# Add and tanh-GELU on one core: one ScalarE pass over z instead of an Abs, a GELU and a VectorE step, with larger rows for the transfers

## The chip, the cores and the metric

The kernel runs on one core of one Trainium2 chip. The metric is the time in microseconds (us) of one execution on the device. Engines are named as the profile names them: DVE is VectorE, ACT is ScalarE, POOL is GpSimd, SP is SyncE, which here only issues DMAs. PE, the matmul engine, has no work.

## The reference

```python
def setup_inputs():
    batch, dim = 1024, 4096
    return {"x": randn(batch, dim) as float32, "y": randn(batch, dim) as float32}

def reference(x, y):
    z = x + y
    return (0.5 * z * (1 + np.tanh(np.sqrt(2 / np.pi) * (z + 0.044715 * z ** 3)))).astype(np.float32)
```

Each input and the output are 16.8 MB, so 50.3 MB move in one execution.

## The kernel before

Each of the 128 partitions holds 8 consecutive rows of the matrices, 32768 fp32 elements or 128 KB. A single tile `z` of that size holds x, then z = x + y, then the result, all in place. y passes through a two-buffer pool of 8192 elements each.

The work is cut into 16 chunks of 2048 elements. For each chunk there are four steps. `add` (line 150) adds y into z, on DVE for the six chunks in `by_dve` and on POOL for the other ten. `mag` (line 155) writes |z| into PSUM on ACT. `gelu` (line 158) replaces it in PSUM by GELU(-|z|), also on ACT. `end` (line 167) adds max(z, 0) and that PSUM tile into z on DVE, by the identity GELU(z) = max(z, 0) + GELU(-|z|). Two PSUM tiles take turns, so `mag` of a chunk waits for `end` of the chunk two before.

All transfers are issued by SP in the order of the list `sp`, and its instructions wait in that order: y0, x0, y1, x1, y2, y3, then three stores. A transfer of y has 8192 elements of each partition (rows of 32 KB, 4 MB in all), one of x 16384 (64 KB, 8 MB); the stores have 16384, 10240 and 6144 (64, 40 and 24 KB). y2 and y3 reuse the two y buffers and wait for the four adds that read the buffer before. The first store waits, beside its own data, for the first half of `end` of chunk 8 (`FIRST`), by a dependency added by hand. The order on POOL, ACT and DVE is written out in the lists `pool`, `acts` and `dve`; each engine works through its list in order.

At the start a one-column activation makes the GELU table load early. `begin_early` moves the first two DMA issues (y0 and x0) ahead of the program's start barrier, and `wait_late` moves the wait for the last store behind the closing barrier; both are the same in the two kernels.

Of the kernel before, what the change touches and what calls it, by code (L numbers as in the profile page):

```python
# [8 lines left out]
def begin_early(nc, count):  # L9


    head, body = (b.instructions for b in nc.main_func.blocks[:2])
    SP = mybir.EngineType.SP
    moved = [i for i in body if i.engine == SP and isinstance(i, mybir.InstDMACopy)][:count]
    assert not any(i.sync_info and i.sync_info.on_wait for i in moved)
    assert all(i.regs_accessed() == ((), ()) for i in moved)
    at = next(k for k, i in enumerate(head) if i.engine == SP)
    for k, i in enumerate(moved):
        body.remove(i)
        head.insert(at + k, i)  # L20


def wait_late(nc):

    body, end = (b.instructions for b in nc.main_func.blocks[1:3])
    last = [i for i in body if isinstance(i, mybir.InstDMACopy)][-1]
    (sem,) = [u.id for u in last.sync_info.on_update]
    all_done = end[0]  # L30
    reset = next(i for i in end if isinstance(i, mybir.InstDrain) and i.is_reset_sema)
    at = end.index(reset)
    clear = end[at + 1]
    first, stop = reset.reset_range_start, reset.reset_range_stop
    assert all_done.engine == mybir.EngineType.SP and reset.engine == mybir.EngineType.Pool
    assert isinstance(clear, mybir.InstISA) and clear.engine == mybir.EngineType.Pool
    waits = all_done.sync_info.on_wait
    (its,) = [w for w in waits if w.id == sem]

    end[0] = mybir.InstDrain(  # L40
        name=all_done.name, engine=all_done.engine, debug=all_done.debug, is_reset_sema=False,
        sync_info=mybir.SyncInfo(on_wait=[w for w in waits if w.id != sem], on_update=[]),
    )
    parts = []
    for f, e in ((first, sem), (sem + 1, stop)):
        if f < e:
            nc.gpsimd.sem_clear(range(f, e))
            parts.append(nc.cur_bb.bb.instructions.pop())
    end[at + 1 : at + 2] = parts
    end.append(  # L50
        mybir.InstEventSemaphore(
            name=clear.name, engine=mybir.EngineType.Activation, debug=clear.debug,
            sync_info=mybir.SyncInfo(
                on_wait=[its],
                on_update=[
                    mybir.SyncUpdate(
                        sync_type="semaphore", id=sem, ant_name=its.ant_name,
                        update_mode="sem-sub-imm", update_value=its.wait_value,
                    )
                ],  # L60
            ),
        )
    )


@with_exitstack
def kernel(
    ctx: ExitStack,
    tc: tile.TileContext,
    x: bass.AP,  # L70
    y: bass.AP,
    out: bass.AP,
):

    nc = tc.nc
    P = nc.NUM_PARTITIONS
    fp32 = mybir.dt.float32
    act = mybir.ActivationFunctionType
    alu = mybir.AluOpType

    N, D = x.shape
    assert N % P == 0
    TOT = N // P * D  # L90
    xv, yv, ov = (a.rearrange("(p n) d -> p (n d)", p=P) for a in (x, y, out))

    YS = 8192
    CH = 2048
    PS = 2
    xloads = [16384, 16384]
    yloads = [8192, 8192, 8192, 8192]
    FIRST = 8
    stores = [16384, 10240, 6144]

    def ranges(sizes):
        ends = [sum(sizes[: i + 1]) for i in range(len(sizes))]
        assert ends[-1] == TOT
        return [(e - f, e) for e, f in zip(ends, sizes)]

    xr, yr, sr, cr = (ranges(r) for r in (xloads, yloads, stores, [CH] * (TOT // CH)))
    C = len(cr)

    by_dve = {0: 0, 2: 0, 4: 2, 6: 4, 8: 8, 12: 10}

    def over(rs, lo, hi):
        return [i for i, (a, b) in enumerate(rs) if a < hi and b > lo]

    pool_sb = ctx.enter_context(tc.tile_pool(name="xz", bufs=1))
    pool_y = ctx.enter_context(tc.tile_pool(name="y", bufs=2))
    pool_w = ctx.enter_context(
        tc.tile_pool(name="w", bufs=PS, space=bass.MemoryType.PSUM)
    )

    one = pool_sb.tile([P, 992], fp32, tag="one", name="one")  # L120
    zt = pool_sb.tile([P, TOT], fp32, tag="z", name="z")
    yt, wt, ends = {}, {}, {}

    def load_x(i):
        a, b = xr[i]
        nc.sync.dma_start(out=zt[:, a:b], in_=xv[:, a:b])

    def load_y(i):
        a, b = yr[i]
        s, o = divmod(a, YS)  # L130
        if o == 0:
            yt[s] = pool_y.tile([P, YS], fp32, tag="y", name=f"y{s}")
        nc.sync.dma_start(out=yt[s][:, o : o + b - a], in_=yv[:, a:b])  # L133

    def store(i):
        a, b = sr[i]
        ins = nc.sync.dma_start(out=ov[:, a:b], in_=zt[:, a:b])
        if i == 0:
            tc.add_manual_dep(
                ins.ins,  # L140
                ends[FIRST].name,
                mybir.DependencyInfo(mybir.DependencyClass.Sync, mybir.DependencyReason.DATA),
                reason="the stores join the queue when the last load is nearly done",
            )

    def add(c):
        a, b = cr[c]
        s, o = divmod(a, YS)
        eng = nc.vector if c in by_dve else nc.gpsimd
        eng.tensor_add(out=zt[:, a:b], in0=zt[:, a:b], in1=yt[s][:, o : o + b - a])  # L150

    def mag(c):
        a, b = cr[c]
        wt[c] = pool_w.tile([P, CH], fp32, tag="w", name=f"w{c}")
        nc.scalar.activation(out=wt[c], in_=zt[:, a:b], func=act.Abs)  # L155

    def gelu(c):
        nc.scalar.activation(  # L158
            out=wt[c], in_=wt[c], func=act.Gelu_apprx_tanh, scale=-1.0
        )  # L160

    def end(c):
        a, b = cr[c]
        parts = 2 if c == FIRST else 1
        n = (b - a) // parts
        for o in range(0, b - a, n):
            ins = nc.vector.scalar_tensor_tensor(  # L167
                out=zt[:, a + o : a + o + n], in0=zt[:, a + o : a + o + n], scalar=0.0,
                in1=wt[c][:, o : o + n], op0=alu.max, op1=alu.add,
            )  # L170
            ends.setdefault(c, ins.ins)


    sp = [(load_y, 0), (load_x, 0), (load_y, 1), (load_x, 1), (load_y, 2), (load_y, 3)]
    sp += [(store, i) for i in range(len(stores))]
    pool = [(add, c) for c in range(C) if c not in by_dve]
    dve, acts = [], []
    for c in range(C):
        dve += [(add, k) for k in sorted(by_dve) if by_dve[k] == c] + [(end, c)]
        acts += [(mag, c), (gelu, c)]  # L180

    needs = {
        load_x: lambda i: [],
        load_y: lambda i: [
            (add, c) for c in over(cr, yr[i][0] - 2 * YS, yr[i][1] - 2 * YS)
        ],
        add: lambda c: [(load_x, i) for i in over(xr, *cr[c])]
        + [(load_y, i) for i in over(yr, *cr[c])],
        mag: lambda c: [(add, c)] + ([(end, c - PS)] if c >= PS else []),
        gelu: lambda c: [(mag, c)],  # L190
        end: lambda c: [(gelu, c)],
        store: lambda i: [(end, c) for c in over(cr, *sr[i])] + [(end, FIRST)],
    }
    queues = [sp, pool, acts, dve]
    done = set()
    with tc.manual_schedule():
        nc.vector.memset(one[:, :1], 0.0)  # L197
        nc.scalar.activation(out=one[:, :1], in_=one[:, :1], func=act.Gelu_apprx_tanh)  # L198
        while any(queues):
            moved = False  # L200
            for q in queues:
                while q and all(n in done for n in needs[q[0][0]](q[0][1])):
                    fn, arg = q.pop(0)
                    fn(arg)
                    done.add((fn, arg))
                    moved = True
                    if q is not sp:
                        break
            assert moved, [q[:1] for q in queues]

    ctx.close()
    tc.close()
    tc.compile()  # L213
    begin_early(nc, 2)
    wait_late(nc)
# [30 lines left out]
```

## Time and profile before

| | before |
|---|---|
| time, median of 3 runs | 119.97 us |
| lowest and highest of the 3 | 119.97 and 120.43 us |
| span of the profiled execution, first to last instruction | 118.5 us |
| time of the profiled execution itself | not listed apart from the three runs; their median lies 1.45 us above its span |
| busy: DVE, ACT, POOL | 59.8, 60.8, 55.5 us |
| DMA queue: bytes, mean rate | 50.33 MB, 425 GB/s |

A line of a group has: the source line, the engine, the operation, what it writes and reads with the shapes, the number of instructions, then busy time and the mean of one in ns, then the idle time of that engine just ahead of these instructions and what ended it. A line of the order in time has: start, duration, engine, source line and operation, and in brackets the idle time before it. A line of waits has: who waited for whom, the sum in us, the number of times, the longest. The DMA line shows the span in 40 equal slices, each digit the busy share of the 16 DMA engines in tenths. A DMA of this kernel is cut into 128 packets, one for each partition's row, 8 for each of the 16 DMA engines; the trace also has each packet's start and duration. All transfers go through one queue.

### The profile page before, as it was taken

Reading aid. Unit: us, or ns where it says so; the run is one execution under the profiler, and the core shown is the slowest. Engines: PE = TensorE matmul, PEld = TensorE weight load, DVE = VectorE, ACT = ScalarE, POOL = GpSimd, SP = SyncE. Lnnn points to the kernel's source line nnn. Section 1 sums busy time; section 2 is a strip of 40 time slices with the busy share of each in tenths; the row PEclk is TensorE's granted clock in tenths of the full one; section 3 lists DMA queues with packets and bytes.
Section 4 is the critical chain, followed back from the end, with each engine's and each line's share of the span. In section 5 each row is a group of like instructions: output and inputs, shape, how many; then the busy total and the mean of one; then the engine's idle time right before and its main releaser. Section 6 shows DMA issues by size and latency. Waiting matters only on the chain.

```text
span 118.5 us, 160 instructions
## 1 busy us (share of the span) xinstructions
DVE 59.8 (50%) x24; ACT 60.8 (51%) x34; POOL 55.5 (47%) x14
## 2 busy tenths in 40 slices
DVE  0000000000399999699994594257999457742000
ACT  5000000000057989999369805797798999940000
POOL 0000000000399999998000029999999999100000
DMA  6989888998889988988899898998899889999996
GB/s 199 509 365 697 354 354 354 663 398 354 354 376 509 531 354 354 686 376 354 354 398 487 365 520 354 531 531 354 354 531 531 354 354 442 442 442 442 390 406 265
DMA packets 1296, 50.33 MB, mean 425 GB/s; under 512 B 144, under 2 KB 144, under 8 KB 144
## 3 DMA queue, kind: packets, MB, share of 16 engines
q1 hardware_dynamic: 1296, 50.33, 98.7%
HBM read 33.55 MB, written 16.78 MB: 425 GB/s over the span
## 4 chain that ended last, share of the span: by engine, by line
DMA 48%; POOL 34%; POOLq 4%; ACT 3%; DVE 2%; issue 0%; SPq 0%; DVEq 0%
POOL z L150 34%; DMA z<-in_x_dram 26%; DMA y<-in_y_dram 21%; POOLq L213 4%; DVE z L167 2%; ACT w L155 2%; ACT w L158 2%; SPq L133 0%; POOLq L150 0%; DVEq L167 0%
## 5 line engine op out<-in xcount | busy, mean ns | idle before, releaser
L150 POOL TENSOR_TENSOR z<-z,y 128x2048 f32<-128x2048 f32 x10 | 55.3, 5556 | 45.6 <-DMA z<-in_x_dram 31.1
L155 ACT ACTIVATE w<-z 128x2048 f32<-128x2048 f32 x16 | 30.1, 1880 | 42.5 <-DVE z L150 36.0
L167 DVE SCALAR_TENSOR_TENSOR z<-z,w 128x2048 f32<-128x2048 f32 (+1 forms) x17 | 36.3, 2155 | 16.0 <-ACT w L158 16.0
L150 DVE TENSOR_TENSOR z<-z,y 128x2048 f32<-128x2048 f32 x6 | 23.9, 4004 | 30.4 <-DMA z<-in_x_dram 30.1
L158 ACT ACTIVATE w<-w 128x2048 f32<-128x2048 f32 x16 | 29.8, 1862 | 0.5
L198 ACT ACT_TABLE_LOAD x1 | 1.3, 1283 | 1.3 <-PEq L230 1.3
L197 DVE MEMSET one<- 128x1 f32 x1 | 0.1, 59 | 1.3 <-PEq L230 1.3
L198 ACT ACTIVATE one<-one 128x1 f32<-128x1 f32 x1 | 0.2, 203 | 0.0
L230 POOL MEMSET const-float32-0.0<- 128x1 f32 x1 | 0.1, 100 | 0.2 <-issue 0.2
L230 POOL MEMSET const-uint8-127<- 128x1 uint8 x1 | 0.1, 103 | 0.0
L230 POOL MEMSET const-bfloat16-1.0<- 128x1 bf16 x1 | 0.1, 102 | 0.0
L230 POOL MEMSET const-float32-1.0<- 128x1 f32 x1 | 0.1, 100 | 0.0
## 6 DMA issues: line engine op xcount, KB each, us to landing
y<-in_y_dram SPq DMA_DIRECT2D x4, 4096.0 KB, 23.6
out_dram<-z SPq DMA_DIRECT2D x1, 5120.0 KB, 14.9
out_dram<-z SPq DMA_DIRECT2D x1, 3072.0 KB, 10.9
z<-in_x_dram SPq DMA_DIRECT2D x2, 44.9
out_dram<-z SPq DMA_DIRECT2D x1, 21.5
```

The source lines that it names most:

```text
L150: eng.tensor_add(out=zt[:, a:b], in0=zt[:, a:b], in1=yt[s][:, o : o + b - a])
L155: nc.scalar.activation(out=wt[c], in_=zt[:, a:b], func=act.Abs)
L158: nc.scalar.activation(out=wt[c], in_=wt[c], func=act.Gelu_apprx_tanh, scale=-1.0)
L167: ins = nc.vector.scalar_tensor_tensor(out=zt[:, a + o : a + o + n], in0=zt[:, a + o : a + o + n], scalar=0.0, in1=wt[c][:, o : o + n], op ...
L197: nc.vector.memset(one[:, :1], 0.0)
L198: nc.scalar.activation(out=one[:, :1], in_=one[:, :1], func=act.Gelu_apprx_tanh)
L213: tc.compile()
L230: nc = _bacc.Bacc("TRN2", target_bir_lowering=False, num_devices=1)
```

## The change

The steps `mag` and `end` are gone. `gelu` is one activation of ScalarE over z itself, from SBUF to SBUF, in place. All adds are on DVE but that of chunk 16, the last 2048 elements, which is on POOL. Of chunks 9 and 10, ACT copies x into PSUM (`to_psum`) when x1 has landed, and their adds on DVE take x from there. The last quarter's chunks are 2048, 2048, 1024, 1024 and 2048 elements, and ACT takes the chunks of the second half in the order 8, 9, 10, 11, 16, 12, 13, 14, 15.

y has one buffer of 16384 elements. y0 and y1 fill its two halves with rows of 32 KB; y2 has rows of 64 KB, fills all of it again, and so waits for adds 0 to 7. The order on SP is y0, y1, x0, x1, y2, store 0, store 1, each store with rows of 64 KB (8 MB). Store 0 waits for gelus 0 to 7 and nothing else (`GATE` is None); store 1 waits for all gelus of the second half. The two issues ahead of the start barrier are now y0 and y1.

```diff
-    YS = 8192
-    CH = 2048
-    PS = 2
-    xloads = [16384, 16384]
-    yloads = [8192, 8192, 8192, 8192]
-    FIRST = 8
-    stores = [16384, 10240, 6144]
+    HALF = TOT // 2
+    xloads = [HALF, HALF]
+    yloads = [8192, 8192, 16384]
+    stores = [16384, 16384]
+    chunks = [2048] * 14 + [1024, 1024, 2048]
+    by_pool = [16]
+    in_psum = [9, 10]
+    GATE = None
...
-    by_dve = {0: 0, 2: 0, 4: 2, 6: 4, 8: 8, 12: 10}
+    second = next(c for c in range(C) if cr[c][0] == HALF)
...
+    yt = pool_y.tile([P, HALF], fp32, tag="y", name="y")
+    xp, adds = {}, {}
...
     def load_y(i):
         a, b = yr[i]
-        s, o = divmod(a, YS)
-        if o == 0:
-            yt[s] = pool_y.tile([P, YS], fp32, tag="y", name=f"y{s}")
-        nc.sync.dma_start(out=yt[s][:, o : o + b - a], in_=yv[:, a:b])
+        o = a % HALF
+        nc.sync.dma_start(out=yt[:, o : o + b - a], in_=yv[:, a:b])
...
+    def to_psum(c):
+        a, b = cr[c]
+        xp[c] = pool_ps.tile([P, 2048], fp32, tag="xp", name=f"xp{c}")
+        nc.scalar.copy(out=xp[c][:, : b - a], in_=zt[:, a:b])
+
     def add(c):
         a, b = cr[c]
-        s, o = divmod(a, YS)
-        eng = nc.vector if c in by_dve else nc.gpsimd
-        eng.tensor_add(out=zt[:, a:b], in0=zt[:, a:b], in1=yt[s][:, o : o + b - a])
-
-    def mag(c):
+        o = a % HALF
+        eng = nc.gpsimd if c in by_pool else nc.vector
+        first = xp[c][:, : b - a] if c in in_psum else zt[:, a:b]
+        ins = eng.tensor_add(out=zt[:, a:b], in0=first, in1=yt[:, o : o + b - a])
+        adds[c] = ins.ins
+
+    def gelu(c):
         a, b = cr[c]
-        wt[c] = pool_w.tile([P, CH], fp32, tag="w", name=f"w{c}")
-        nc.scalar.activation(out=wt[c], in_=zt[:, a:b], func=act.Abs)
-
-    def gelu(c):
-        nc.scalar.activation(
-            out=wt[c], in_=wt[c], func=act.Gelu_apprx_tanh, scale=-1.0
-        )
-
-    def end(c):
...
+        nc.scalar.activation(out=zt[:, a:b], in_=zt[:, a:b], func=act.Gelu_apprx_tanh)
 
-    sp = [(load_y, 0), (load_x, 0), (load_y, 1), (load_x, 1), (load_y, 2), (load_y, 3)]
+    sp = [(load_y, i) for i in over(yr, 0, HALF)] + [(load_x, 0), (load_x, 1)]
+    sp += [(load_y, i) for i in over(yr, HALF, TOT)]
     sp += [(store, i) for i in range(len(stores))]
-    pool = [(add, c) for c in range(C) if c not in by_dve]
-    dve, acts = [], []
-    for c in range(C):
-        dve += [(add, k) for k in sorted(by_dve) if by_dve[k] == c] + [(end, c)]
-        acts += [(mag, c), (gelu, c)]
+    pool = [(add, c) for c in by_pool]
+    dve = [(add, c) for c in range(C) if c not in by_pool]
+    order = [8, 9, 10, 11, 16, 12, 13, 14, 15]
+    acts = [(gelu, c) for c in range(second)] + [(to_psum, c) for c in in_psum]
+    acts += [(gelu, c) for c in order]
...
```

## The prediction

> **What bounds the kernel now.** I read the page's engine shares first, then its DMA line and queue.
>
> ```profile
> span 118.5 us, 160 instructions
> DVE 59.8 (50%) x24; ACT 60.8 (51%) x34; POOL 55.5 (47%) x14
> DMA  6989888998889988988899898998899889999996
> q1 hardware_dynamic: 1296, 50.33, 98.7%
> ```
>
> No engine is busy for much over half of the span; the one DMA queue is busy for 98.7% of it. The view of the DMA issues by line, one window for each issue, gives issue plus time to landing: y0 12.1, x0 0.43+31.0=31.4, y1 1.26+39.9=41.2, x1 1.64+58.8=60.4, y2 44.75+25.4=70.2, y3 57.99+21.8=79.8, and the stores 77.60+21.5=99.1, 96.32+14.9=111.2 and 107.55+10.9=118.5, the end of the span. The landings are 19.3 us apart for each 8 MB and 9.7 for each 4 MB: the queue never ran dry. In the packet records a row of 64 KB takes 2.418 us, 32 KB 1.213, 40 KB 1.514, 24 KB 0.912, with 16 in flight; the last packet ends at 118.13 and the span 0.40 later.
>
> The queue's own waits come next.
>
> ```profile
> SPq L133 <- DVE z L150: 51.0, 2, 38.2
> SPq L137 <- DVE z L167: 48.4, 3, 19.2
> ```
>
> SyncE waits long for the adds and the ends, but ahead of need: y2 is issued 15 us before the queue reaches it, y3 11 us. The shortest lead is the first store's: issued at 77.60, while the 16 engines end y3 between 78.99 and 79.45. With 1.39 to 1.85 us of lead, no packet shows a gap over 0.01 us. The chain of waits runs through POOL and ends at 107.5, 11 us early; the queue sets the end.
>
> For costs, the groups by form:
>
> ```profile
> L150 POOL TENSOR_TENSOR z<-z,y 128x2048 f32<-128x2048 f32 x10 | 55.3, 5556 | 45.6 <-DMA z<-in_x_dram 31.1 <-DMA y<-in_y_dram 14.5
> L155 ACT ACTIVATE w<-z 128x2048 f32<-128x2048 f32 x16 | 30.1, 1880 | 42.5 <-DVE z L150 36.0 <-DVE z L167 3.9 <-POOL z L150 2.6
> L158 ACT ACTIVATE w<-w 128x2048 f32<-128x2048 f32 x16 | 29.8, 1862 | 0.5
> L198 ACT ACTIVATE one<-one 128x1 f32<-128x1 f32 x1 | 0.2, 203 | 0.0
> ```
>
> And the order in time, between 33 and 45 on DVE, then near 70 (start, duration):
>
> ```profile
> 33.75 6.58 DVE L150 TENSOR_TENSOR z<-z,y 128x2048 f32<-128x2048 f32 x1
> 40.25 4.47 DVE L167 SCALAR_TENSOR_TENSOR z<-z,w 128x2048 f32<-128x2048 f32 x2
> 44.65 2.28 DVE L150 TENSOR_TENSOR z<-z,y 128x2048 f32<-128x2048 f32 x1
> 70.22 2.29 DVE L150 TENSOR_TENSOR z<-z,y 128x2048 f32<-128x2048 f32 x1 [0.22 <-DMA y<-in_y_dram]
> 70.26 6.61 POOL L150 TENSOR_TENSOR z<-z,y 128x2048 f32<-128x2048 f32 x1 [14.49 <-DMA y<-in_y_dram]
> ```
>
> A DVE add alone takes 2.28. Beside a GpSimd add one of the two waits out the other: DVE's second add took 6.58, GpSimd's take 6.61, against 4.50 undisturbed. The two ends from 40.25 read PSUM for one operand, and kept 2.2 us each beside a running GpSimd add.
>
> **What falls away, at nothing.** Sixteen Abs passes, sixteen ends (36 us of DVE) and nine GpSimd adds go. All lies beside a queue that never stopped, so none of it shortens the end. The bytes stay. By the row times, with 8 rows per engine and DMA, y's second half and the second half of the stores in 64 KB rows save 8x(2x1.213-2.418) + 8x(1.514+0.912-2.418) = 0.06+0.06, some 0.1 us. That is all there is to gain. Loading y0 and y1 first and x0 third only reorders a full queue (x0 is issued after the start barrier, near 1.3, and needed at 21): x0 and y1 together still land at 41.1 (y1's landing now), x1 at 60.4.
>
> **First new wait: y2.** It now loads 8 MB over the whole y buffer, so it waits for all of adds 0 to 7, all on DVE. DVE starts 0.1 after the landing, at 41.2. Starts of back-to-back DVE operations lie 2.20 apart (40.25 and 44.65 are two apart), so the eighth add ends at 41.22 + 7x2.20 + 2.28 = 58.9; the queue issued 0.03 after its releaser in before, so y2 is issued at 58.97. The engines end x1 between 59.63 and 60.09 (as now): a lead of 0.66 to 1.12, below any seen to suffice. Queued behind y2 on SyncE is only store 0, which is ready at 61 (one gelu after the last add) and needed at 80.
>
> **Second new wait: store 1.** It covers the whole second half, and needs every gelu of it. Counting from T, when DVE starts on the landed y2: add 8 first, GpSimd's add 16 behind it in the shared port until T+6.65, exactly the rows at 70.22 and 70.26. Adds 9 and 10 take x from PSUM, which I cost as the ends from 40.25 (nearest row, one PSUM operand): no contention, starts at T+2.2 and T+4.4. Add 11 starts at T+6.6, as GpSimd gets out of the way, and ends at T+8.89. Its gelu starts at T+8.92. From there ACT is late, not DVE: 11, 16, 12, 13, then two halves 14 and 15. A large gelu from SBUF to SBUF is not in the trace. A pass from PSUM to PSUM takes 1.86 and from SBUF to PSUM 1.88, so SBUF at one end costs 0.02; I take another 0.02 for the other end: 1.90. Starts lie 1.77 apart where a pass need not wait for the one before it (51.84 and 53.61 in the timeline), 1.91 where it does (53.61 and 55.52). These gelus don't wait for each other: 1.80, with 1.77 and 1.94 as ends. Between one column (203 ns) and 2048 (1880) lies 0.82 ns a column, so a half chunk takes 1.04 and its follower starts 0.96 after it. The sum to the issue is 8.92 + 4x1.80 + 0.96 + 1.04 + 0.03 = 18.15 after T, between 18.0 and 18.85. DVE's last add ends before that, at T+15.6. Store 0 meanwhile runs 19.3 us from y2's end, which is T-0.45 (x0's last packet ended at 31.09, DVE started at 31.54). So store 1 is issued some 0.7 us before store 0 has ended: again too short a lead.
>
> The Trainium skill ("ScalarE: Activation LUTs", The pipeline for one element) says that ScalarE reaches PSUM faster than SBUF, which speaks against moving the gelu to SBUF. Its figure for a [128,1] bias operand, 280 ns + 0.833 N, would make the pass 1.99 and the chain an estimated 0.5 us longer; the trace's 1.88 for a pass that reads SBUF does not agree with that figure, and no row here has a large SBUF output.
>
> The copies to PSUM (two of 1.9) run from 61 to 65 on ACT, after gelu 7 and long before y2 lands near 80: nothing, while that gap lasts; without it, up to 3.8 in front of gelu 8. Should Copy need another function table, two loads of 1.28 fit there too.
>
> **Price of a short lead.** Call L the time from an issue to the point from which the stream runs at full rate, on the slowest engine. Cold, in this trace: y0 issued at 0, first packets at 1.01 to 1.85, last packet at 11.77 where 8x1.21 = 9.68 is streaming, so L = 2.09. Lower end: 1.01, the first packet of all. From the side, store 0's lead of 1.39 to 1.85 left no gap, so L in a warm queue is hardly above 1.4 to 1.8. The chain is then: y2 issued 58.97, ends 58.97+L+19.32, T is 0.45 later, store 1 is issued 18.15 later, and ends L+19.32 after that; with the 0.40 at the end, span = 116.6 + 2L. Below L = 1.12 the slowest engine is still on x1, and it is 117.7 + L; with no loss at all 118.4, the old sum less 0.1. L = 1.01 gives 118.7, L = 1.4 gives 119.4, L = 2.09 gives 120.8. I take L = 1.5, nearest to the first store, with a little for a stream that has truly stopped: 119.6. The profiled execution's own time is not listed apart from the three runs; their median 119.97 lies 1.45 above the span of 118.5, and the change leaves what surrounds the span alone. So 119.6 + 1.45 is 121.1.
>
> The Trainium skill ("DMA: Bandwidth & Descriptors", Specifications) gives a first-byte latency of about 0.6 us for DMAs that SyncE issues. By it both leads would just do, and the time would be an estimated 119.9; the first packet at 1.01 after its issue in this trace does not agree, though that one was cold.
>
> **Rivals.** (1) Not slower: the queue refills within the leads, and the stream has no hole. Decided at L below about 1.25 (span 119.1, time 120.57, the upper edge of what counts as no change); with full cover 119.9. For it speak the two small deficits, 0.3 to 0.7 us each; against it the start of the span. (2) GpSimd gets the port first when y2 lands. Then add 8 waits 4.5, every later gelu too, and the time is 121.1 + 4.5 = 125.6. Against it: DVE started first all three times in this trace (31.54, 44.65, 70.22), by 0.04 us. A PSUM add that does contend costs the same. (3) Store 0, in the queue from 61 with no gate now, shares the engines with y2 instead of waiting behind it: eight y2 rows with seven store rows between them end at 60.5+15x2.42 = 96.8, then 0.5 + 18.15 + 1.5 + 19.3 + 0.4 + 1.45, 138. Against it: one queue, whose DMAs landed in the order of issue.
>
> **How the numbers follow.** 0.5% (0.6 us) is about what a measurement of this kernel can tell from no change. Forecast, two holes, 120.6 to 122.4: 0.65. Rival 1: 0.25, nearly all within 0.5%. Rival 2 with the PSUM variant: 0.05. Rival 3: 0.02. The rest, 0.03, is faster by more, for which the 0.1 us of row times leaves no reason but an error of mine. The ACT bounds of 18.0 to 18.85 move the time by -0.15 to +0.7, and L at 2.09 gives 122.2: range 120.0 to 122.6. Faster 0.03, same 0.25, slower 0.72.
>
> **What would show it.** In the profile after: adds 0 to 7 from 41.2 at 2.2 pitch; y2's issue near 59.0; a hole in the DMA slices near 60 and another near 99; y2 landing at 79.8 to 80.7, 8 MB of stores at 19.3 us each; DVE's add 8 ahead of GpSimd's; ACT busy without a gap from add 11's gelu on; the last issue 18.15 after T. Wrong: no holes (rival 1), a second load under way with stores at 62 (rival 3), or a span below 118.3.

## The result, and the profile after

The change makes the kernel slower: 123.08 us median of six runs against 119.97, a ratio of 1.0241 (95% interval 1.0211 to 1.0271). The forecast was 121.1 with a range of 120.0 to 122.6, so the direction was right and the size was missed by about 2 us. The profiled execution took 124.88, 2.1% above the fastest of the six, and the ratio leaves it out. The other five lie between 122.33 and 123.80, and a second profile of the same kernel follows below (122.0 of span, 123.48).

The page of the changed kernel, engine shares and DMA:

```profile
span 123.4 us, 101 instructions
DVE 33.3 (27%) x17; ACT 35.3 (29%) x21; POOL 6.8 (6%) x5
DMA  9897989779977977797979988979989927797777
q1 hardware_dynamic: 1008, 50.33, 96.5%
```

DVE, ACT and POOL lost 26.5, 25.5 and 48.7 us of work, and the span grew by 4.9. The queue moves the same 50.33 MB, and is busy for 96.5% of a longer span instead of 98.7%. The "2" in the slices marks a hole that was not there before: the engines end store 0 between 100.4 and 103.4, and store 1's packets begin at 103.5.

The queue's own waits:

```profile
SPq L132 <- ACT z L156: 42.9, 2, 41.4
SPq L128 <- DVE z L151: 37.2, 1, 37.2
```

These are the two new waits that the prediction named: y2 waits for the adds, store 1 for the gelus. Then the groups, with forms of the same operation and tiles merged:

```profile
L156 ACT ACTIVATE z<-z 128x2048 f32<-128x2048 f32 (+1 forms) x17 | 30.2, 1805 | 66.1 <-DVE z L151 66.1
L151 POOL TENSOR_TENSOR z<-z,y 128x2048 f32<-128x2048 f32 x1 | 6.6, 6622 | 84.1 <-DMA y<-in_y_dram 84.1
L151 DVE TENSOR_TENSOR z<-xp,y 128x2048 f32<-128x2048 f32 x2 | 4.5, 2282 | 0.0
L144 ACT COPY xp<-z 128x2048 f32<-128x2048 f32 x2 | 3.7, 1858 | 0.0
```

The adds from PSUM take 2.28 each beside a running GpSimd add, as costed. In order of time, the stretches that set the end (three dots stand for rows left out):

```profile
41.19 17.70 DVE L151 TENSOR_TENSOR z<-z,y 128x2048 f32<-128x2048 f32 x8 [39.80 <-DMA z<-in_x_dram]
58.92 0.33 SPq L128 DMA_DIRECT2D y<-in_y_dram  x1
...
84.50 2.29 DVE L151 TENSOR_TENSOR z<-z,y 128x2048 f32<-128x2048 f32 x1 [25.61 <-DMA y<-in_y_dram]
84.57 6.62 POOL L151 TENSOR_TENSOR z<-z,y 128x2048 f32<-128x2048 f32 x1 [84.13 <-DMA y<-in_y_dram]
86.71 4.48 DVE L151 TENSOR_TENSOR z<-xp,y 128x2048 f32<-128x2048 f32 x2
91.11 8.96 DVE L151 TENSOR_TENSOR z<-z,y 128x2048 f32<-128x2048 f32 x5
93.42 9.20 ACT L156 ACTIVATE z<-z 128x2048 f32<-128x2048 f32 x6 [0.29 <-DVE z L151]
```

y2 is issued at 58.92 (forecast 58.97). DVE starts on it at T = 84.50, where the forecast had 80.2. The last gelu ends at 102.62 and store 1 is issued at 102.65, that is T+18.15, the forecast to the hundredth. So everything on DVE, ACT and GpSimd went as reckoned, and the loss is in y2: 25.5 us from issue to landing for 19.3 us of streaming.

```profile
y<-in_y_dram SPq DMA_DIRECT2D x1, 25.5
```

The packet records say where. First, y2's first packets begin 0.98 to 2.67 us after the issue, and its first rows of 64 KB take 2.63 to 3.44 us instead of 2.42; the slowest engine comes to full rate 3.70 after the issue. Second, which no step of the prediction has: each engine's last row of y2, near 77 to 80, takes long, 1.4 us more on average and 4.22 instead of 2.42 on the engine that ends last. Behind these rows lies store 0, in the queue since 60.86.

### The profile page after: what moved, and what is told of

Read it like the earlier page. It is cut to its first block, busy times and chain, and to the rows that moved or that the text cites. A ratio compares the mean times of both kernels' runs of the same rounds, so it can differ in the third digit from the quotient of the medians.

```text
span 123.4 us, 101 instructions
## 1 busy us (share of the span) xinstructions
DVE 33.3 (27%) x17; ACT 35.3 (29%) x21; POOL 6.8 (6%) x5
## 2 busy tenths in 40 slices
DMA packets 1008, 50.33 MB, mean 408 GB/s; under 512 B 112, under 2 KB 112, under 8 KB 112
## 3 DMA queue, kind: packets, MB, share of 16 engines
q1 hardware_dynamic: 1008, 50.33, 96.5%
## 4 chain that ended last, share of the span: by engine, by line
DMA 53%; DVE 20%; ACT 7%; DVEq 2%; ACTq 1%; issue 0%
DMA z<-in_x_dram 32%; DMA y<-in_y_dram 21%; DVE z L151 20%; ACT z L156 7%; DVEq L198 2%; ACTq L198 1%; DVEq L151 0%
## 5 line engine op out<-in xcount | busy, mean ns | idle before, releaser
L156 ACT ACTIVATE z<-z 128x2048 f32<-128x2048 f32 (+1 forms) x17 | 30.2, 1805 | 66.1 <-DVE z L151 66.1
L151 DVE TENSOR_TENSOR z<-z,y 128x2048 f32<-128x2048 f32 (+1 forms) x14 | 29.0, 2133 | 65.4 <-DMA z<-in_x_dram 39.8
L151 POOL TENSOR_TENSOR z<-z,y 128x2048 f32<-128x2048 f32 x1 | 6.6, 6622 | 84.1 <-DMA y<-in_y_dram 84.1
L151 DVE TENSOR_TENSOR z<-xp,y 128x2048 f32<-128x2048 f32 x2 | 4.5, 2282 | 0.0
L144 ACT COPY xp<-z 128x2048 f32<-128x2048 f32 x2 | 3.7, 1858 | 0.0
## 6 DMA issues: line engine op xcount, KB each, us to landing
y<-in_y_dram SPq DMA_DIRECT2D x1, 25.5
```

The source lines that it names most:

```text
L144: nc.scalar.copy(out=xp[c][:, : b - a], in_=zt[:, a:b])
L151: ins = eng.tensor_add(out=zt[:, a:b], in0=first, in1=yt[:, o : o + b - a])
L156: nc.scalar.activation(out=zt[:, a:b], in_=zt[:, a:b], func=act.Gelu_apprx_tanh)
```

## The experiments

The theory that this profile suggests has two parts. **Restart**: y2 meets a queue about to run out and comes up late. **Turn**: a store that waits in the queue behind the loads makes their last rows slow. The rivals: chance stalls, a store whose issue disturbs y2's start, a cost of the new compute, two equal holes as forecast. In this table "landing" is issue to landing of the last large load of y (y2, or y3 where there are four). Each ratio is to runs of the kernel before on the same chip, where its median was 119.97 to 120.16. In the edits, three dots stand for lines left out.

| kernel | landing, us | time, median | ratio to before (95%) |
|---|---|---|---|
| e0, the change again | 24.2 | 122.93 | 1.0222 (1.0182 to 1.0263) |
| e1, store 0 at 64.3 | 24.1 | 123.21 | 1.0245 (1.0204 to 1.0287) |
| e2, y in four loads | 22.0 | 121.15 | 1.0076 (1.0051 to 1.0100) |
| e3, store 1 in two | 23.2 | 122.85 | 1.0227 (1.0176 to 1.0277) |
| e4, e2 and store 0 at 77.4 | 21.4 | 120.16 | 1.0003 (0.9986 to 1.0020) |
| e5, e2 and store 0 at 72.5 | 22.0 | 121.05 | 1.0076 (1.0057 to 1.0095) |
| e6, store 0 at 78.8 by a clock | 24.0 | 122.63 | 1.0181 (1.0146 to 1.0216) |
| e7, before without its gate | 23.1 | 121.09 | 1.0076 (1.0057 to 1.0095) |
| e8, y2 with 3 us of lead | 21.3 | 120.44 | 1.0031 (1.0014 to 1.0048) |
| e9, y2 into a dry queue | 21.8 | 126.87, one run | |
| e10, no PSUM, no GpSimd | 23.6 | 124.35 | 1.0340 (1.0290 to 1.0389) |
| e11, e2 and store 0 at 74.6 | 21.9 | 120.97, one run | |
| e12, y2 at 60.7 | 23.1 | 124.18 | 1.0332 (1.0300 to 1.0365) |
| e13, e12 again | 23.0 | 124.25, one run | |

**e0_again**: no edit.

> The changed kernel once more, unedited, for a second look at y2's start. Restart theory: a load that is handed to a queue with about 0.9 us of work left finds it dry; first packets begin between 1.0 and 2.7 us after the issue, on single engines late, and each first row of 64 KB takes 0.5 to 1.0 us longer than the 2.42 us of the others, so that the last engine is 3 to 4 us behind the issue: DVE's second-half start T near 82 to 83, span near 121.5. Chance theory (a stall of all engines in the middle of y2, as the row times of 3.4 to 4.3 us near 77 to 80 in the first profile of the change): rows of y2 other than the first are long again only now and then; without such rows T would be near 82 and the span near 121.

The order in time of this second profile, from T:

```profile
83.11 2.29 DVE L151 TENSOR_TENSOR z<-z,y 128x2048 f32<-128x2048 f32 x1 [24.30 <-DMA y<-in_y_dram]
101.26 0.34 SPq L132 DMA_DIRECT2D out_dram<-z  x1
```

T+18.15 again. The first rows near 60 are long again (up to 3.29), and so are all sixteen last rows, 3.33 to 4.23. Chance would hardly repeat both. On the engine that ends last, full rate came 2.68 after the issue and the last row cost 1.81.

**e1_store0_late**: store 0 also waits for the second copy to PSUM.

```diff
-        if i == 0 and GATE is not None:
+        if i == 0:
             tc.add_manual_dep(
                 ins.ins,
-                adds[GATE].name,
+                copies[10].name,
...
```

> Store 0 is issued only after the second copy to PSUM, near 64.4 us instead of 60.9, still 15 us before the queue needs it. Store theory (the issue of store 0 two microseconds behind y2's delays the descriptors of y2's last engines): y2's last first packet begins near 60.6 instead of 61.6, T falls by about 1 us or more, span near 120.3. Restart theory: nothing changes, T 82 to 83, span 121.5.

Issued at 64.28, it changed nothing: first packets 0.97 to 2.02 after y2's issue, landing 24.1. Store 0's issue does not disturb y2's start. The long last rows stayed as well; the store was issued 13 us before they began.

**e2_y_quarters**

```diff
-    yloads = [8192, 8192, 16384]
+    yloads = [8192, 8192, 8192, 8192]
```

> y's second half in two loads of 4 MB with rows of 32 KB: the first waits for adds 0 to 3 only and is issued near 50.2, ten us ahead of need, the second near 58.9 with 10 us of lead. Chunks 8 to 11 then start near 70.2 and store 1 is ready early too, so both holes go. Restart theory: no gap in the packets anywhere, span 118.5, time 119.9 to 120.0, as before. If the changed compute cost anything by itself (the in-place pass over SBUF, DVE's adds beside the transfers), the span would stay above 119.5.

The landing of y3 in this kernel:

```profile
y<-in_y_dram SPq DMA_DIRECT2D x1, 4096.0 KB, 22.0
```

The hole near 60 is gone (no row there differs from 1.21) and with it 1.8 us, but the time is 121.15, not the 119.95 expected. Neither the restart nor the compute explains the rest: from 76.5 on, the last two rows of y3 on every engine are long, 1.0 us together on average. This miss made the turn theory.

**e3_stores_split**

```diff
-    stores = [16384, 16384]
+    stores = [16384, 8192, 8192]
```

> Store 1 in two stores of 4 MB with rows of 32 KB: the first waits for gelus 8 to 11 and is issued near T+10.8, the second for the rest, 10 us ahead of need; the hole before store 1 goes, that before y2 stays. Theory of two like holes (the prediction, 1.5 us from issue to full rate at each): span 0.8 us shorter than the changed kernel's. Restart theory with a short start for stores (0.85 to 1.0 us from issue to the first packets, full rate at once, in the first profile of the change) and the last engine of y2 setting T: on that engine store 0 ends at T+18.9 and store 1's rows began at T+19.1, so only 0.2 to 0.3 us are to be had.

T in this profile, whose span is 120.8:

```profile
82.20 2.29 DVE L151 TENSOR_TENSOR z<-z,y 128x2048 f32<-128x2048 f32 x1 [23.29 <-DMA y<-in_y_dram]
```

The time is 122.85 against the change's 122.93 on the same chip (e0). The four runs of each spread over 0.9 to 1.2 us, so the times alone would hardly show 0.8. From T to the end of the span, where y2's unsteady start is left out, this kernel takes 38.6 us (120.8 less 82.20), and the change and e0 38.9 each. So the hole before store 1 is worth 0.3 us, not the 0.8 of two equal holes. In the packet records of the change a store is fast to start: store 1's packets begin 0.85 to 1.0 us after its issue and run at full rate at once.

**e7_before_ungated**: the kernel before, without its dependency of the first store on `ends[FIRST]`.

```diff
+    GATE = False
...
-        if i == 0:
+        if i == 0 and GATE:
             tc.add_manual_dep(
...
-        store: lambda i: [(end, c) for c in over(cr, *sr[i])] + [(end, FIRST)],
+        store: lambda i: [(end, c) for c in over(cr, *sr[i])],
```

> The kernel before with only its hand-made dependency taken out: the first store is issued when its own data is ready, near 70.0 us, instead of at 77.6. Turn theory: y3's last rows near 77 to 80 become long, span 119.7, time 121.1, although no engine's work is different. Chance theory: 119.97 as before.

In order of time and in the view of DMA issues, the first store and y3 of the kernel before:

```profile
77.60 0.35 SPq L137 DMA_DIRECT2D out_dram<-z  x1
```
```profile
y<-in_y_dram SPq DMA_DIRECT2D x1, 4096.0 KB, 21.8
```

And of this kernel:

```profile
69.83 0.35 SPq L138 DMA_DIRECT2D out_dram<-z  x1
```
```profile
y<-in_y_dram SPq DMA_DIRECT2D x1, 4096.0 KB, 23.1
```

y3 lands 23.1 after its issue, 21.8 in the kernel before; its last two rows are 1.0 us longer on average, and the kernel loses 0.9 us (1.0076, against 120.16 on the same chip) although no load, no compute and no byte differs. This is the turn by itself. It takes a store behind a load: in the kernel before, y2 waits 15 us in the queue behind x1, and x1's last rows take 2.42 like the others; in e3 the first half of store 1 waits 7 us behind store 0, whose rows all take 2.42.

**e4_quarters_gate10** and **e5_quarters_gate8** and **e11_quarters_gate9**: e2 with store 0 held by the adds' own progress (`GATE` is 10, 8 and 9).

```diff
-    GATE = None
+    GATE = 10
```

> The kernel with y in four loads of 32 KB rows, and its store 0 held until add 10 is done, near 76.9 us, 2.1 to 2.6 us before the last load ends. Turn theory (a store that lies in the queue behind the loads before their last rows start makes those rows slow on every engine, some 1.2 us lost; seen as long rows near 77 to 80 in the change and all its variants so far, and not in the kernel before, which holds its first store): the long rows shrink or go, span 118.5 to 118.8, time 119.9 to 120.3. Chance or fixed-time theory (a stall at that time of the execution, whatever the queue holds): they stay, time 121.1.

> The same with store 0 held only until add 8, near 72.5 us, 6.5 us before the last load ends. Turn theory: the store is there well before the last rows start, so the loss is whole again: long rows, span 119.7, time 121.1. If only a lead of 15 us and more did harm, it would be 119.9 to 120.

> y in four loads of 32 KB rows, store 0 held until add 9, near 74.8: between the 72.5 that lost 1 us and the 77.4 that lost none. In the profiles with the loss it is the rows that start from 76.5 on that are long, so a store whose first descriptors are there by 75.8 should still lose all of it: long rows, span 119.5. If the loss grows with the lead, about half.

The issue of store 0 in e4, and the landing of its y3:

```profile
77.37 0.35 SPq L132 DMA_DIRECT2D out_dram<-z  x1
```
```profile
y<-in_y_dram SPq DMA_DIRECT2D x1, 4096.0 KB, 21.4
```

Issued 2.3 to 2.7 us before the loads end, the store costs nothing: no row near the end takes over 0.1 us more than the usual 1.21, and the time equals before (1.0003). Issued at 72.5 or at 74.6 it costs about 1 us, and the cost does not grow with the lead: 0.9 to 1.0 us more in the last two rows, whether the store is issued 19, 10, 7.7 or 5.5 us before the loads end (e2, e7, e5, e11), which is 15.6 to 1.9 us before the first long row begins. It is there or not, according to whether the store is in the queue when the last 64 KB of load on each engine begin; e4's engines began these between 0.13 us before the issue and 0.25 after it. The chance theory fails here, and so does that of a fixed time. e4 is also the changed compute, all of it, at before's time: the single pass, the adds on DVE and the PSUM copies cost nothing and gain nothing, within the 0.2 us of the interval.

**e6_timer**: the change with e1's dependency and a clock of repeated copies.

```diff
...
+        for n in [2048] * (8 if c == 10 else 1) + [1024] * (c == 10):
+            copies[c] = nc.scalar.copy(out=xp[c][:, :n], in_=zt[:, a : a + n]).ins
...
```

> The changed kernel with y2 as it is, but ACT repeats the second copy to PSUM (7 more whole ones and a half) as a clock, and store 0 waits for the last of them, near 78.2 us, when y2's last rows have begun. Turn theory: y2's last rows take 2.42 us again instead of 3.3 to 4.3, T falls by 1.2 to 1.8 us, span near 120.2, time near 121.7; the long first rows at 60 stay. Chance theory: as the change, span 121 to 122.

Store 0's issue (with store 1's, in one row) and T:

```profile
78.77 22.70 SPq L132 DMA_DIRECT2D out_dram<-z  x2
82.97 2.29 DVE L152 TENSOR_TENSOR z<-z,y 128x2048 f32<-128x2048 f32 x1 [24.08 <-DMA y<-in_y_dram]
```

Half a miss. Store 0 went out at 78.77, and fifteen of sixteen engines, which began their last row by 77.92, took 2.43 us for it; y2 ends on average at 80.28, against 81.32 in e0. But one engine had started y2 only at 61.34; its last row began at 79.20, 0.43 us after the store's issue, and took 3.34. DVE waits for the slowest engine, so T is 82.97, and the time gains only 0.3 to 0.5 us over e0 (by medians, and by the ratios 1.0181 and 1.0222). The turn is cured on the average; the engine that the restart made latest, with 0.9 us of turn on top, then sets T.

**e8_lead3**: y2 needs one add less, the rest of y is a small load; store 0 by the clock.

```diff
-    yloads = [8192, 8192, 16384]
+    yloads = [8192, 8192, 14336, 2048]
...
```

> y's second half as 14336 and 2048 elements a partition (rows of 56 and 8 KB): the first load waits for adds 0 to 6 only and is issued near 56.7, 2.9 to 3.4 us before the 16 engines run out, the rest near 58.9; store 0 waits for a clock of copies on ACT and is issued near 77.0, some 2.4 us before the last load ends. Restart and turn theories together: no long rows at 60 nor at 77, span 118.5 to 118.8, time 119.9 to 120.3. If a load needs more than 3 us of lead, long first rows stay at 60 and the span is 119.5 to 121.

Issued at 56.54, 3.0 to 3.4 us before the engines run out, no row of y2 takes over 0.3 us more than the rest; the last engine ends it 0.5 behind the mean. The time is 120.44, 0.3% above before: 2.6 of the 3.1 us are back, and 3 us of lead is nearly enough, 10 (e2, e4) quite.

**e9_dry**, **e12_y2_later**, **e13_y2_later_again**: y2 waits for more than it needs, in e9 for the copy that ends at 64.4, in e12 and e13 for gelu 7. In e9 store 0 is held by a clock of copies, as in e6; in e12 and e13 nothing but its data holds it. The edit shown is that of e12 and e13.

```diff
+        if i == 2:
+            tc.add_manual_dep(
+                ins.ins,
+                gelus[7].name,
...
```

> y2 is held until the second copy to PSUM ends, near 64.4, when the queue has been dry for 4 us; store 0 waits for a clock of copies near 84. If the late start of single engines comes from meeting x1's last packets, the first packets begin 1.0 to 1.85 us after the issue as at the start of the execution, the slowest engine at full rate after 2.1 us. If every restart is like that of y2, single engines begin 2.0 to 2.7 us after the issue, and the slowest is at full rate after 2.7 to 3.7 us. Either way the first rows are 0.5 to 1.0 us long; the span is near 125.

> The changed kernel with y2 held until gelu 7 is done, near 60.86, 0.6 us after x1's last packet, and 1.9 us later than in the change; store 0 follows at once, so the long last rows stay. If meeting x1's last packets is what starts single engines late, the first packets begin 0.95 to 1.7 us after the issue, the slowest engine is at full rate 2.1 to 2.2 us after it, y2 lands about 23.4 us after its issue and the span is 122.6 to 123.2, with less spread than the change's. If single engines start late in any restart that comes soon, the slowest engine needs 2.1 to 3.7 us and the spans are 123 to 125.

> The same kernel for a second profile: the same two expectations for the first packets of y2 and for its landing.

The landing of y2 in e9, then its issue and landing in e12:

```profile
y<-in_y_dram SPq DMA_DIRECT2D x1, 21.8
```
```profile
60.69 0.33 SPq L128 DMA_DIRECT2D y<-in_y_dram  x1
```
```profile
y<-in_y_dram SPq DMA_DIRECT2D x1, 23.1
```

e9 is a restart alone: first packets 0.96 to 1.63 after the issue, first rows 0.25 to 1.03 longer than 2.42, the slowest engine at full rate after 2.2, 21.8 in all, as at the start of the execution (2.09). e12 and e13, issued 0.7 to 0.8 us after x1's last packet, look the same at the start (0.96 to 1.50, slowest engine 2.0 and 2.1) and have the turn's 1.2 to 1.3 on top. The change's y2, issued 0.65 to 1.3 us before x1's engines run out, has a last engine that begins 1.7 to 2.7 after the issue, and full rate after 2.1 to 3.7 (six profiles: the change, e0, e1, e3, e6, e10). At the start of the execution, in all sixteen profiles, full rate came after 1.9 to 2.15; five of the six are beyond all the starts into an empty queue, e3 is not. Also, e12's four runs lie within 0.2 us, the change's six within 2.6. So a load handed over in the last microsecond mostly starts worse, and less evenly, than one handed to an empty queue. Why single engines come late there, the records do not show. Issuing later does not pay: what is won at the start is less than the wait.

**e10_plain_adds**

```diff
-    by_pool = [16]
-    in_psum = [9, 10]
+    by_pool = []
+    in_psum = []
...
-    order = [8, 9, 10, 11, 16, 12, 13, 14, 15]
+    order = [8, 9, 10, 11, 12, 13, 14, 15, 16]
```

> The changed kernel with all adds on DVE from SBUF, no copies to PSUM, nothing on GpSimd, chunks in their order. If the reckoning from T holds (DVE's starts 2.20 apart, a last gelu of 1.91), store 1 is issued at T+19.7 instead of T+18.15, and the span is 1.5 us above the changed kernel's. If the shared port of GpSimd and DVE mattered more than the rows show, it would be nearer.

T is 82.64 there, and the end of the order in time reads:

```profile
100.45 1.91 ACT L156 ACTIVATE z<-z 128x2048 f32<-128x2048 f32 x1 [0.67 <-DVE z L151]
102.39 0.34 SPq L132 DMA_DIRECT2D out_dram<-z  x1
```

T+19.75 (expected 19.7), and 1.3 to 1.4 us more time than the change (123.08) and e0 (122.93); from T to the end of the span it is 40.5 us against 38.9. Once T sets the end, the copies to PSUM and the one GpSimd add are worth what the reckoning gave them.

## Why the prediction was right or wrong

**Right.** The queue bounds the kernel, and all the removed work was worth nothing: e4, with the compute changed and the queue kept fed, takes before's time. Both new waits are where they were put. The adds from 41.2, y2's issue (58.92; the sum's own terms give 58.93, not the 58.97 written), DVE's add ahead of GpSimd's, the PSUM adds, the gelu of 1.89 to 1.91 at starts 1.80 apart and T+18.15 came within 0.1 us. Rival 2 did not happen in any profile. What the Trainium skill ("ScalarE: Activation LUTs", Step-by-step: what each stage is for) says of PSUM, that ScalarE writes there faster than to SBUF, agrees in direction, by 0.01 to 0.03 us: 1.88 for the Abs pass from SBUF to PSUM before, 1.89 to 1.91 for the GELU from SBUF to SBUF after.

**Wrong: the price of a short lead for y2.** The step took L = 1.5 with 2.09 as its end, "nearest to the first store". The first store is a store, and a store needs about 1.0 from issue to full rate; for a load the nearest row was the start of the execution, 2.09, which e9, e12 and e13 repeat (2.0 to 2.2). And even that was no upper end, since a lead that just misses gave 2.1 to 3.7 on the slowest engine. The term that was to be 1.5 measured 2.7 in e0 and 3.7 in the first profile. For store 1 the same L was too dear by 0.5. Why single engines come late after a near miss stays open.

**Wrong: the edit that was costed at nothing.** "Queued behind y2 on SyncE is only store 0, which is ready at 61 and needed at 80." The kernel before holds that store by hand until 77.6, and the change drops the dependency. The prediction read the first store's short lead as a limit, and not as something that a kernel may want. The early store costs 0.9 to 1.4 us on the average engine, and 1.7 to 1.8 on the one that ended last in the change, in e0 and in e1. Rival 3 had the place and the direction, the store meeting the load in the queue, but spread it over all of y2 and priced it at 17 us; it reaches only the last 64 KB of load per engine.

**The sum, for e0.** From the forecast span of 119.6: +1.18 for y2's L (2.68 for 1.5), +1.81 for the turn, -0.5 for store 1's L, -0.13 for an issue at 58.84 instead of 58.97, together 121.96; its span was 122.0. The error was not in the chain but in these terms: L, too cheap for the load and too dear for the store, and the turn, which was missing. The bounds did not cover it, as both unknowns were bounded by rows of another kind: a load by a store, and an early store by nothing.

## What to carry to other kernels

In a kernel that is bound by one full DMA queue, faster engines buy nothing; ask of each edit only when it makes the next transfer ready, and on the slowest of the 16 engines. Give a load several microseconds of lead (3 nearly did here, 10 did), for instance by splitting a transfer so that its first part needs less. Do not let the first store into the queue behind the loads early: hold it until some 2 us before the last load ends, and when a kernel has such a hand-made hold, price its removal.

## What the runs showed of the hardware

- A store queued behind loads slows the last 64 KB of load on each engine by 0.9 to 1.0 us on average (rows of 32 KB: e2, e5, e7, e11) or 1.1 to 1.4 (rows of 64 KB: the change, e0, e1, e3, e10, e12, e13), if it was issued before these rows begin. It costs nothing if it comes 2.3 to 2.7 us before the loads end (e4) or 1.4 to 1.9 (before). Where the limit lies is known only roughly: engines that began their last 64 KB up to 0.25 us after the issue were spared (e4), one that began 0.43 us after it was not (e6).
- A load queued behind a load, and a store behind a store, slow nothing (before, e3).
- The Trainium skill ("DMA: Bandwidth & Descriptors", Two DMAs through the same engine are not ordered) says that descriptors of a queue start in order but are pipelined, with the read and the write side of an engine as separate queues. A store that begins to read while the last load rows are still being written would fit the long rows; no run here shows that this is the cause.
- First packets of a DMA into an empty queue begin 0.85 (a store) to 1.0 us after the issue, and those of a load on the last engine 1.4 to 1.85. A load is at full rate after 1.9 to 2.2, since its first rows take up to 1.1 us more than the rest; a store after 1.0. The same skill page (Specifications) gives about 0.6 us to the first byte; no first packet here came before 0.8 from the start of the issue on SyncE. The issue itself takes 0.33 to 0.38 us there, so from its end it is 0.5 (a store) to 0.65 us, near the page's figure.
- A load issued 0.65 to 1.3 us before the queue runs out came up later on single engines in four of six profiles (2.0 to 2.7 to the last first packet) than any load issued into an empty queue (1.4 to 1.85: e9, e12, e13 and the start of every execution).
